# SSD scan of a hybrid encoder step: decay rows spread over the partitions by transfers from DRAM instead of matmuls, the decay matrix clamped and formed in place, the mask moved into the score block

## The chip, the cores and the metric

The kernel runs on one core of a Trainium2 chip. The metric is the device time of one execution in microseconds; it is given as the median of three runs. The engines are named as in the profile: PE (TensorE matmuls), PEld (TensorE weight loads), DVE (VectorE), ACT (ScalarE), POOL (GpSimd) and SP (SyncE, which issues the DMAs here).

## The reference, cut to what matters

The program is one inference step of a two-layer encoder: a Mamba-2 state-space (SSD) mixer with its FFN, then band attention with its FFN, in fp32, on 1024 prompt and 64 sample tokens of width 1024. Only the scan of the first layer is touched:

```python
dA = dt * A                                   # per token and head
Acs = jnp.cumsum(dA, axis=-1)                 # within a chunk
Lm = jnp.exp(jnp.where(causal, Acs[..., :, None] - Acs[..., None, :], -jnp.inf))
CB = jnp.einsum('bcqgn,bcsgn->bcgqs', Cc, Bc)
y_diag = jnp.einsum('bcgjqs,bcsgjp->bcqgjp', CB[:, :, :, None] * Lm, xd)
decay_to_end = jnp.moveaxis(jnp.exp(Acs[..., -1:] - Acs), -1, 2)
chunk_states = jnp.einsum('bcsgn,bcsgjp->cbgjpn', Bc, xd * decay_to_end[..., None])
h_final, h_prev = lax.scan(step, h0, (chunk_states, chunk_decay))   # h * d + s
y_off = jnp.einsum('bcqgn,cbgjpn->bcqgjp', Cc, h_prev) * jnp.moveaxis(jnp.exp(Acs), -1, 2)[..., None]
y = y_diag + y_off
```

There are 32 heads of 64 channels in 4 groups that share B and C, and a state of 128.

## The kernel before, in words

**Tiling.** The 1088 tokens are cut into three slices of 384, 384 and 320 columns, and a slice into chunks of 128 (nine in all, the last one of 64). Heads go in 16 pairs j, so a pair's 128 channels fill the partitions. A pair on a slice is a *unit* of the scan, numbered q = 3j + s: 48 units, 32 of 384 columns and 16 of 320.

**Main loop.** PE is filled by the input projection: tile by tile (z, x, B, C), eight k-steps of three passes, 24 matmuls in PSUM tile `mm` (L451 to L453), whose result DVE scales and moves out (`zs`, `craw`, L728). From x come the convolution and Silu (`xsT`, L766 to L776).

**Side tasks.** `table_task` (L683) makes the tables of dt and of the running sums `acs`, transposes the sums (`acT`, L715) and puts them as high and low parts into the rows `acr`; `cd` and `dec` are exponentials of them. `group_task` (L781) makes `Bn` and the score block `CB` of a group, copied from PSUM by ACT (L799). `ssd_task` (L809) is one unit: transposes `xtp` (L823); `xd` on DVE (L833), `xe` on POOL (L834); for each of the two heads a matmul `bcp` (L840) that spreads the head's row of running sums over all partitions (a selector column as weights, `acr` as the moving side); on DVE three operations that subtract the partition's own sum and take the minimum with a mask (L845); Exp of 64 rows for the state part (`ea`, L849) and of the matrix `dm` (L850) on ACT; `dm` times `CB` on DVE (L851). Then `sp`, the chunk states (L859), the state recurrence `hn` (L869, L872), `yp` from `dm` and `xd` (L889), `yo` from the states (L898), and the sum `y` (L900 to L903), which POOL multiplies by the gate z (L910) and SP stores to DRAM (L911). After a group's four pairs the sums of squares `ssg` (L921) are transposed (`nst`, L484) into a norm.

**What sets the order.** PE's order is written out by hand: a planner with a clock of its own (class `Stream`) lets main matmuls run, and puts a side task's next piece between them when its delay is over and its condition holds; a yield is (cost, delay, condition). So `SSD_D` and the numbers in the yields decide how many main matmuls stand between a unit's pieces. A tile of x is emitted only when the scan is near enough (L1077 and the lines after it: `so["C"] > q - 5`). The order on DVE, ACT, POOL and SP is made by the tile scheduler from priorities and buffers; each of these engines, and SP's queue, then takes its instructions strictly in order.

Of the kernel before, what the change touches and what calls it, by code (L numbers as in the profile page):

```python
# [8 lines left out]
F32 = mybir.dt.float32  # L9
F32R = mybir.dt.float32r  # L10
# [28 lines left out]

GAP_A, GAP_B = 1.8, 1.2  # L40
# [3 lines left out]
SSD_GAP, SSD_D = 4.4, 6.5  # L44
# [328 lines left out]
def hybrid_kernel(  # L373
# [34 lines left out]
    yd_ = dr.tile([P, XT, T], F32, name="yscr")  # L408
    od_ = dr.tile([P, KD, T], F32, name="oscr")
# [225 lines left out]
    with ExitStack() as es:  # L635
        pbc = es.enter_context(tc.tile_pool(reuse_waits="tile", name="pbc", bufs=2, space=PSUM))
        pyy = es.enter_context(tc.tile_pool(reuse_waits="tile", name="pyy", bufs=2, space=PSUM))
# [6 lines left out]
        mask = sb1.tile([P, P], F32, name="mask")  # L644
        G.memset(mask, BIG)
        G.affine_select(mask, mask, pattern=[[1, P]], compare_op=ALU.is_ge, fill=-BIG, base=0, channel_multiplier=-1)
# [3 lines left out]
        sel = sb1.tile([P, 32], F32R, name="sel")  # L650
        zero = sb1.tile([P, 1], F32, name="zero")
        G.memset(zero, 0.0)
        V.tensor_copy(sel[64:128, :], zero[64:128, :].to_broadcast([64, 32]))
        V.tensor_copy(sel[0:64, :], stk)
# [6 lines left out]
        acr = sb1.tile([P, T], F32R, name="acr")  # L661
        A.copy(acr[64:128, :], zero[64:128, :].to_broadcast([64, T]))
# [12 lines left out]
        dt, acs, dec, cd = tab("dt"), tab("acs"), tab("dec"), tab("cd")  # L675
# [7 lines left out]
        def table_task():  # L683
            ps = ax("dtn")
            for c in range(NCH):
                PE.matmul(ps[:, c * 32:(c + 1) * 32], dtT[c // 3][:64, (c % 3) * P:(c % 3 + 1) * P], stk, start=True, stop=True)
            with tc.high_priority(HIP):
                tt_ = [sb2.tile([P, 3, P], F32, tag=tg, bufs=2, name="tt") for tg in ("xe", "xe")]
                t0, t1 = (fl(t_)[:, :HW].rearrange("p (a b) -> p a b", b=HEADS) for t_ in tt_)
                t3 = dec  # L690
                V.tensor_tensor(t0, ps[:, :HW].rearrange("p (a b) -> p a b", b=HEADS), hb(pbs[:, 0:32]), op=ALU.add)
                V.scalar_tensor_tensor(fl(t1), fl(t0), -1.0, fl(t0), op0=ALU.mult, op1=ALU.min)
                A.activation(fl(t1), fl(t1), AF.Exp)
                V.tensor_scalar(fl(t3), fl(t1), LP[-1], None, op0=ALU.mult)
# [4 lines left out]
                V.scalar_tensor_tensor(t0, dt, -1.0, hb(negA), op0=ALU.mult, op1=ALU.mult)  # L699
            yield 1.0, TB_V  # L700
            pa = ax("acsp")
            PE.matmul(pa[:, :HW], U, fl(t0), start=True, stop=True)
            with tc.high_priority(HIP):
                V.tensor_copy(fl(acs), pa[:, :HW])
            yield 0.5, 1.0
            pl_ = ax("lastp")
            PE.matmul(pl_[:, :HW], ones, fl(t0), start=True, stop=True)

            with tc.high_priority(HIP):
                for s, (o, n) in enumerate(SL):  # L710
                    ps = (pyy, pyy, pbc)[s].tile([P, 512], F32, tag=("yy", "yy", "bc")[s], name="acT")
                    for i in range(3):
                        c = 3 * s + i
                        L = CHL[c]
                        PE.transpose(ps[:32, i * P:i * P + L], acs[:L, c, :], ident[:L, :L])  # L715
# [22 lines left out]
        class Conv:  # L738
# [5 lines left out]
            def __call__(self, s, ps_):  # L744
# [26 lines left out]
                if s < 2:  # L771
                    A.activation(dst[:, :384], dst[:, :384], AF.Silu)
# [8 lines left out]
        def group_task(g, s):  # L781
# [27 lines left out]
        def ssd_task(j, s):  # L809
# [5 lines left out]
            yield 0, 0, lambda: tabs and (g, s) in cb_done and so["A"] == q and so["C"] >= q - 1 and st.t >= so["tA"]  # L815
# [19 lines left out]
            MT = []  # L835
            ea = sb2.tile([P, 384], F32, tag="ea", name="ea")
            for e in range(2):
                hh = 2 * j + e
                bp = pbc.tile([P, 512], F32, tag="bc", name="bcp")
                PE.matmul(bp[:, :n], sel[:, hh:hh + 1].to_broadcast([P, P]), acr[:, o:o + n], start=True, stop=True)  # L840
                dm = sb2.tile([P, 384], F32, tag="dm", bufs=4, name="dm")
                for i in range(3):
                    c = 3 * s + i
                    L = CHL[c]
                    V.scalar_tensor_tensor(  # L845
                        dm[:, i * P:i * P + L], bp[:, i * P:i * P + L], acs[:, c, hh:hh + 1], mask[:, :L],
                        op0=ALU.subtract, op1=ALU.min,
                    )
                A.activation(ea[64 * e:64 * e + 64, :n], bp[64 * e:64 * e + 64, :n], AF.Exp)  # L849
                A.activation(dm[:, :n], dm[:, :n], AF.Exp)  # L850
                V.tensor_tensor(dm[:, :n], dm[:, :n], CB[:, :n], op=ALU.mult)  # L851
# [34 lines left out]
            for i in range(3):  # L886
                L = CHL[3 * s + i]
                for e in range(2):
                    PE.matmul(  # L889
                        yp[64 * e:64 * e + 64, i * P:i * P + L], xd[:, i, 64 * e:64 * e + 64],  # L890
                        MT[e][:, i * P:i * P + L], start=True, stop=True,
# [30 lines left out]
            if jj == 3:  # L922
                yield 0, 5.0
# [6 lines left out]
        def evac_of(kind, i):  # L930
# [32 lines left out]
        tags = [[], [("dm", 4)] * 4 + [("y", 6)] * 3 + [("ea", 2)], [("ea", 2)] + [("CT", 5)] * 2 + [("xd", 2)] * 2]  # L963
        for s, (o, n) in enumerate(SL):
# [14 lines left out]
            for m in range(KD):  # L979
                if m < len(tags[s]):  # L980
# [55 lines left out]
        for s in range(NSL):  # L1036
            us, n = u[s], SL[s][1]
            pl, tg = (pyy, "yy") if s == 1 else (pbc, "bc")
# [947 lines left out]
```

## Time and profile before

| | |
|---|---|
| Median of 3 runs | 2995.19 us (2993.03 to 2996.16) |
| Profiled execution | 2997.29 us, of which the span is 2995.6 us |
| Mean granted TensorE clock | 0.994 |
| Busy: PE, PEld | 2948.2 us (98%), 2891.8 us (97%) |
| Busy: DVE, ACT, POOL | 2044.8 us (68%), 1460.1 us (49%), 699.0 us (23%) |
| Scan's part of the span | about 87 to 660 us |

A row of the trace's timeline gives the start, the duration in us, engine, line, operation, `out<-in`, and how many instructions it sums up; what stands in brackets is idle time before it and who ended it. A row of the groups gives busy time and the mean in ns, then the idle time before. A row of waits gives the engine and its line, whom it waited for, us in total, how often, and the longest. Matmuls overlap, so a row's duration is longer than the distance to the next.

### The profile page before, as it was taken

To read this page: it belongs to the slowest core of one execution; us is meant where nothing else is said; L and a number is where in the kernel's file an instruction comes from. 1 tells how busy PE (TensorE), PEld (TensorE's weight loads), DVE (VectorE), ACT (ScalarE), POOL (GpSimd) and SP (SyncE) were. 2 spreads that over 40 slices of the span, in tenths; PEclk is the share of its full clock that TensorE was granted. 3 is DMA by queue.
4 is the path that set the end of the run, shared out by engine and by line. 5 is a ranking of instruction groups with operands and counts; after the bars stand their busy time and mean duration, and the time that the engine had idled before them with its cause. 6 is when DMAs were issued, how large, how long until landed. Compare 5 with 4: busy or idle time off the path is not lost.

```text
span 2995.6 us, 56513 instructions
## 1 busy us (share of the span) xinstructions
PE 2948.2 (98%) x21722; PEld 2891.8 (97%) x21722; DVE 2044.8 (68%) x4512; ACT 1460.1 (49%) x2643; POOL 699.0 (23%) x848
## 2 busy tenths in 40 slices
PE   8999999999999999999999999999999999999999
PEld 7999999999999999999999899999899999999999
DVE  7778887885768554574557778777778655475544
ACT  6756566564453232244445566555654322244443
POOL 1333333330121433351111000000131343451111
PEclk9999999999999999999999999999999999999999
DMA  3011111124654222255655222222356222245654
GB/s 122 33 59 51 61 50 49 61 68 145 192 150 141 83 73 80 76 161 173 202 177 169 87 76 79 70 65 86 116 171 188 80 76 77 80 148 176 214 179 136
DMA packets 180671, 335.43 MB, mean 112 GB/s; under 512 B 18192, under 2 KB 128400, under 8 KB 180400
## 3 DMA queue, kind: packets, MB, share of 16 engines
q1 hardware_dynamic: 178608, 325.45, 34.3%
q0 software_dynamic: 1792, 6.36, 1.1%
q8 instruction: 171, 2.80, 0.4%
q14 instruction: 100, 0.82, 0.1%
HBM read 264.69 MB, written 62.60 MB: 109 GB/s over the span
## 4 chain that ended last, share of the span: by engine, by line
PE 88%; DVE 7%; DMA 2%; ACT 2%; issue 1%; POOL 0%; SPq 0%; DVEq 0%; ACTq 0%; POOLq 0%
PE px L1264 9%; PE px L1265 9%; PE px L1266 9%; PE mm L451 8%; PE mm L453 8%; PE mm L452 8%; PE po L1464 6%; PE po L1465 6%; PE po L1463 6%; PE mmx L452 3%; PE mmx L451 3%; PE mmx L453 3%; PE po L1747 2%; PE ptp L1708 1%; PE yp L889 1%
## 5 line engine op out<-in xcount | busy, mean ns | idle before, releaser
L451 PE MATMUL mm<-r,hl 128*128 128x384 f32 (+2 forms) x1664 | 554.3, 333 | 6.4 <-DVE dt L698 3.4
L453 PE MATMUL mm<-r,hl 128*128 128x384 f32 (+2 forms) x1664 | 539.9, 324 | 3.2 <-DVE hl L351 2.6
L452 PE MATMUL mm<-r,hl 128*128 128x384 f32 (+2 forms) x1664 | 539.0, 324 | 0.0
L339 DVE TENSOR_TENSOR hl<-raw,hl 128x1024 fp32r<-128x1024 f32 (+1 forms) x219 | 260.6, 1191 | 219.9 <-ACT hl L338 217.3
L1265 PE MATMUL px<-r,hl 128*128 128x288 f32 (+1 forms) x1184 | 348.0, 294 | 0.0
L451 PEld LDWEIGHTS mm<-r,hl 128*128 128x128 f32 x1664 | 315.9, 190 | 9.0 <-ACT BT L775 3.7
L453 PEld LDWEIGHTS mm<-r,hl 128*128 128x128 f32 x1664 | 314.8, 189 | 4.6 <-DVE hl L351 3.7
L452 PEld LDWEIGHTS mm<-r,hl 128*128 128x128 f32 x1664 | 316.1, 190 | 0.0
L1264 PE MATMUL px<-r,hl 128*128 128x288 f32 x1056 | 311.3, 295 | 0.1
L1266 PE MATMUL px<-r,hl 128*128 128x288 f32 x1056 | 311.1, 295 | 0.0
L338 ACT CAST hl<-raw 128x1024 fp32r<-128x1024 f32 (+1 forms) x219 | 219.0, 1006 | 179.9 <-PE po L1465 97.1
L477 POOL TENSOR_TENSOR ssum<-ssum,sq 128x256 f32<-128x256 f32 (+3 forms) x97 | 128.4, 1324 | 640.6 <-ACT sq L476 625.3
L1265 PEld LDWEIGHTS px<-r,hl 128*128 128x128 f32 x1184 | 222.7, 188 | 0.0
L1266 PE MATMUL px<-rx,hl 128*128 128x256 f32 x768 | 216.5, 282 | 4.9 <-DVE hl L339 4.9
L1264 PE MATMUL px<-rx,hl 128*128 128x256 f32 x768 | 217.0, 283 | 0.6 <-ACT hl L338 0.6
L1464 PE MATMUL po<-rx,hl 128*128 128x384 f32 (+1 forms) x624 | 201.7, 323 | 0.1
L1264 PEld LDWEIGHTS px<-r,hl 128*128 128x128 f32 x1056 | 198.7, 188 | 0.5 <-DVE u L1279 0.5
L1266 PEld LDWEIGHTS px<-r,hl 128*128 128x128 f32 x1056 | 198.5, 188 | 0.0
L1463 PE MATMUL po<-rx,hl 128*128 128x384 f32 (+1 forms) x608 | 197.6, 325 | 0.0
L1465 PE MATMUL po<-rx,hl 128*128 128x384 f32 (+1 forms) x608 | 196.7, 323 | 0.0
L1265 PE MATMUL px<-rx,hl 128*128 128x256 f32 x640 | 180.1, 281 | 0.0
L288 POOL TENSOR_TENSOR tt<-raw 128x512 f32<-128x512 f32 x40 | 53.7, 1343 | 439.3 <-DMA raw<-in_w_f_dram 382.8
(367 smaller groups left out, 8163.3 us busy)
## 6 DMA issues: line engine op xcount, KB each, us to landing
raw<-in_w_f_dram SPq DMA_DIRECT2D x154, 512.0 KB, 3.8
rx<-in_w_f_dram SPq DMA_DIRECT2D x54, 512.0 KB, 3.6
raw<-in_w_in_dram SPq DMA_DIRECT2D x40, 512.0 KB, 3.5
sg<-hscr SPq DMA_DIRECT2D x88, 192.0 KB, 3.6
raw<-in_w_f_dram SPq DMA_DIRECT2D x44, 384.0 KB, 3.2
raw<-in_w_so_dram SPq DMA_DIRECT2D x32, 512.0 KB, 3.7
raw<-in_w_kv_dram SPq DMA_DIRECT2D x18, 512.0 KB, 3.5
raw<-in_w_o_dram SPq DMA_DIRECT2D x16, 512.0 KB, 3.6
```

The source lines that it names most:

```text
L338: self.nc.scalar.copy(h, v)
L339: (eng or self.eng or self.nc.vector).tensor_tensor(lo, v, h, op=ALU.subtract)
L451: PE.matmul(ps[:, :n], h_, xh, start=(first and i == 0), stop=False)
L452: PE.matmul(ps[:, :n], h_, xl, start=False, stop=False)
L453: PE.matmul(ps[:, :n], l_, xh, start=False, stop=(last and i == nk - 1))
L477: (eng or G).tensor_tensor(ssum[:, :n], ssum[:, :n], q[:, :n], op=ALU.add)
L1264: PE.matmul(ps, wh, ah[:, k, :], start=(k == 0), stop=False)
L1265: PE.matmul(ps, wh, al[:, k, :], start=False, stop=False)
L1266: PE.matmul(ps, wl, ah[:, k, :], start=False, stop=(k == 3))
L1463: PE.matmul(ps[:, :n], wh, xh, start=(k == 0), stop=False)
L1464: PE.matmul(ps[:, :n], wh, xl, start=False, stop=False)
L1465: PE.matmul(ps[:, :n], wl, xh, start=False, stop=(k == FT - 1))
```

## The change

The running sums are kept with the sign turned (`nac`). Their transposes are copied into rows by ACT and stored to a DRAM scratch `ascr` (32 heads by 1152). A unit then loads its two rows straight from there, spread over all 128 partitions (MT) and over 64 partitions each (`ea`). DVE forms the matrix in place, subtracting the partition's own sum and clamping at 0; ACT takes one Exp of the whole MT and one of `ea`, with a scale of −1. `CB` is multiplied by the triangular 0/1 mask `U` when DVE moves it out of PSUM, and MT by `CB` in one operation. The planner's numbers and the pools change with it.

```diff
-SSD_GAP, SSD_D = 4.4, 6.5
+SSD_GAP, SSD_D = 4.4, 8.0
...
+    ac_ = dr.tile([HEADS, NCH * P], F32, name="ascr")
...
-        pbc = es.enter_context(tc.tile_pool(reuse_waits="tile", name="pbc", bufs=2, space=PSUM))
-        pyy = es.enter_context(tc.tile_pool(reuse_waits="tile", name="pyy", bufs=2, space=PSUM))
+        pyy = es.enter_context(tc.tile_pool(reuse_waits="tile", name="pyy", bufs=4, space=PSUM))
...
-                        PE.transpose(ps[:32, i * P:i * P + L], acs[:L, c, :], ident[:L, :L])
-                    A.copy(acr[0:32, o:o + n], ps[:32, :n])
-                    V.tensor_tensor(acr[32:64, o:o + n], ps[:32, :n], acr[0:32, o:o + n], op=ALU.subtract)
-                V.tensor_tensor(fl(dec), pl_[:, :HW], fl(acs), op=ALU.subtract)
-                A.activation(fl(cd), pl_[:, :HW], AF.Exp)
+                        PE.transpose(ps[:32, i * P:(i + 1) * P], nac[:, c, :], ident)
+                    row = sb2.tile([P, 384], F32, tag="xd", name="row")
+                    A.copy(row[:32, :], ps[:32, :384])
+                    nc.sync.dma_start(ac_[:, o:o + 384], row[:32, :])
+                V.tensor_tensor(fl(dec), fl(nac), pl_[:, :HW], op=ALU.subtract)
+                A.activation(fl(cd), pl_[:, :HW], AF.Exp, scale=-1.0)
...
-                    G.memset(dst[:, 320:384], 0.0)
+                    A.activation(dst[:, 320:384], ident[:, 0:64], AF.Copy, scale=0.0)
...
-                L = CHL[3 * s + i]
-                PE.matmul(ps[:, i * P:i * P + L], BT[:, i * P:(i + 1) * P], CT[:, i * P:i * P + L], start=True, stop=True)
-            A.copy(CB[:, :n], ps[:, :n])
+                sl = slice(i * P, (i + 1) * P)
+                PE.matmul(ps[:, sl], BT[:, sl], CT[:, sl], start=True, stop=True)
+            V.tensor_tensor(
+                CB.rearrange("p (a b) -> p a b", b=P), ps[:, :384].rearrange("p (a b) -> p a b", b=P),
+                U.unsqueeze(1).to_broadcast([P, 3, P]), op=ALU.mult,
+            )
...
-            yield 0, 0, lambda: tabs and (g, s) in cb_done and so["A"] == q and so["C"] >= q - 1 and st.t >= so["tA"]
+            yield 0, 0, lambda: tabs and so["C"] >= q - 3
+            MT = sb2.tile([P, 2, 384], F32, tag="bp", bufs=4, name="MT")
+            row = ac_.offset + 2 * j * NCH * P + o
+            nc.sync.dma_start(MT, bass.AP(ac_.tensor, row, [[0, P], [NCH * P, 2], [1, 384]]))
+            ea = sb2.tile([P, 384], F32, tag="ea", bufs=3, name="ea")
+            for e in range(2):
+                nc.sync.dma_start(ea[64 * e:64 * e + 64, :n], bass.AP(ac_.tensor, row + e * NCH * P, [[0, 64], [1, n]]))
+            m3 = MT[:, :, :n]
+            for e in range(2):
+                for i in range(3):
+                    c = 3 * s + i
+                    m_ = MT[:, e, i * P:i * P + CHL[c]]
+                    last = V.tensor_scalar(m_, m_, nac[:, c, 2 * j + e:2 * j + e + 1], 0.0, op0=ALU.subtract, op1=ALU.max)
+            A.activation(m3, m3, AF.Exp, scale=-1.0)
+            x = A.activation(ea[:, :n], ea[:, :n], AF.Exp, scale=-1.0)
+            tc.add_manual_dep(x.ins, last.ins.name, AT, reason="one table load")
+            yield 0, SSD_D, lambda: (g, s) in cb_done and so["A"] == q and so["C"] >= q - 1 and st.t >= so["tA"]
...
-                PE.matmul(bp[:, :n], sel[:, hh:hh + 1].to_broadcast([P, P]), acr[:, o:o + n], start=True, stop=True)
...
-                A.activation(ea[64 * e:64 * e + 64, :n], bp[64 * e:64 * e + 64, :n], AF.Exp)
-                A.activation(dm[:, :n], dm[:, :n], AF.Exp)
-                V.tensor_tensor(dm[:, :n], dm[:, :n], CB[:, :n], op=ALU.mult)
-                MT.append(dm)
+            V.tensor_tensor(m3, m3, CB[:, :n].unsqueeze(1).to_broadcast([P, 2, n]), op=ALU.mult)
...
-            yield 0.7, 4.5, lambda: so["B"] == q
+            yield 0.35, 6.0, lambda: so["B"] == q
...
-                yield 0, 5.0
+                yield 0, 12.0 if g < 3 else 5.0
...
-                    st.spawn(ssd_task(i, s), SSD_D)
+                    st.spawn(ssd_task(i, s))
```

The rows `acr`, the selector `sel` and the additive `mask` are gone, and the staging tiles of the first layer's input take other buffers.

**How the order moves at the start of the scan.** First PE, from the transposes of units 0 and 1 to the third unit's, in the kernel before. `_1000`, `_1055` and `_1151` number the `xtp` tiles of units 0, 1 and 2; at each "..." 24 main matmuls are left out.

```order
L823 MATMUL xtp_1000<-ident_77,xsT_537 128x128 x3
L840 MATMUL bcp_1009<-acr_145,sel_134 128x384
L840 MATMUL bcp_1018<-acr_145,sel_134 128x384
...
L823 MATMUL xtp_1055<-ident_77,xsT_749 128x128 x3
L840 MATMUL bcp_1064<-acr_145,sel_134 128x384
L840 MATMUL bcp_1073<-acr_145,sel_134 128x384
L859 MATMUL sp_1082<-xe_1005,Bn_626 128x128 x3
...
L889 MATMUL yp_1122<-dm_1011,xd_1004 64x128
L889 MATMUL yp_1122<-dm_1020,xd_1004 64x128
```

In the changed kernel the same place on PE reads as follows, from its first row to its last without a main matmul between; 48 main matmuls of 384 columns and 24 of 320 stand between `acT` and the first `xtp`.

```order
L835 MATMUL xtp_1110<-ident_77,xsT_521 128x128 x3
L835 MATMUL xtp_1124<-ident_77,xsT_733 128x128 x3
L854 MATMUL sp_1133<-xe_1115,Bn_622 128x128 x3
L884 MATMUL yp_1145<-MT_1026,xd_1114 64x128 x6
L893 MATMUL yo_1152<-CT_510,hn_1137 128x128
L893 MATMUL yo_1152<-CT_510,hn_1139 128x128
L854 MATMUL sp_1159<-xe_1129,Bn_862 128x128 x3
L835 MATMUL xtp_1174<-ident_77,xsT_834 128x128 x3
```

The `bcp` rows are gone, and the two tiles of main matmuls that stood between the pieces of units 0 and 1 now stand ahead of them.

Next, SP at the same time in the changed kernel. `row` are the transposed sums of one slice, MT_987, MT_1000, MT_1013 and MT_1026 the matrices of units 1, 2, 3 and 0.

```order
L252 DMA raw_802<-in_w_in_dram 128x1024
L710 DMA ascr_109<-row_942 32x384
L710 DMA ascr_109<-row_949 32x384
L814 DMA MT_987<-ascr_109 128x2x384
L817 DMA ea_989<-ascr_109 64x384
L710 DMA ascr_109<-row_956 32x384
L817 DMA ea_989<-ascr_109 64x384
L814 DMA MT_1000<-ascr_109 128x2x384
L817 DMA ea_1002<-ascr_109 64x320 x2
L814 DMA MT_1013<-ascr_109 128x2x384
L817 DMA ea_1015<-ascr_109 64x384 x2
L814 DMA MT_1026<-ascr_109 128x2x384
```

Before, SP went from the weight rows `raw` straight to the stores of `y`; now three stores and these loads stand between, unit 0's matrix last.

Last, DVE in the changed kernel, from the last main tile ahead of the scan to the product that unit 0's `yp` reads.

```order
L721 TENSOR_TENSOR zs_1107<-mm_1082,rb2_145 128x320
L845 TENSOR_TENSOR xd_1114<-xtp_1110,dt_133 128x384
L845 TENSOR_TENSOR xd_1128<-xtp_1124,dt_133 128x384
L823 TENSOR_SCALAR MT_1026<-MT_1026,nac_134 128x128 x6
L864 COPY hn_1137<-sp_1133 128x128
L847 TENSOR_TENSOR MT_1000<-MT_1000,CB_963 128x2x320
L867 SCALAR_TENSOR_TENSOR hn_1139<-hn_1137,cd_136,sp_1133 128x64 x2
L867 SCALAR_TENSOR_TENSOR hn_1142<-hn_1139,cd_136,sp_1133 128x64 x2
L847 TENSOR_TENSOR MT_1013<-MT_1013,CB_623 128x768
L847 TENSOR_TENSOR MT_1026<-MT_1026,CB_623 128x768
```

Before, each unit's subtractions and products stood right behind its own `xd`; here the products of units 2 and 3 stand ahead of unit 0's.

More of the change, by code (lines that the diff above doesn't have):

```diff
@@ L38 @@
 EPS = 1e-6
+AT = mybir.DependencyInfo(mybir.DependencyClass.Sync, mybir.DependencyReason.DATA)
 GAP_A, GAP_B = 1.8, 1.2
@@ L673, in hb @@
             return ap.unsqueeze(1).to_broadcast([P, NCH, HEADS])
-        dt, acs, dec, cd = tab("dt"), tab("acs"), tab("dec"), tab("cd")
+        dt, nac, dec, cd = tab("dt"), tab("nac"), tab("dec"), tab("cd")
         tabs = []
@@ L703, in table_task @@
             with tc.high_priority(HIP):
-                V.tensor_copy(fl(acs), pa[:, :HW])
+                V.tensor_copy(fl(nac), pa[:, :HW])
             yield 0.5, 1.0
@@ L710, in table_task @@
                 for s, (o, n) in enumerate(SL):
-                    ps = (pyy, pyy, pbc)[s].tile([P, 512], F32, tag=("yy", "yy", "bc")[s], name="acT")
+                    ps = pyy.tile([P, 512], F32, tag="yy", name="acT")
                     for i in range(3):
@@ L834, in ssd_task @@
             G.tensor_tensor(hd(xe), hd(xd), tb(dec), op=ALU.mult)
[L835 to L851, printed above, removed]
-                MT.append(dm)
+            V.tensor_tensor(m3, m3, CB[:, :n].unsqueeze(1).to_broadcast([P, 2, n]), op=ALU.mult)
             so["A"] = q + 1
             so["tA"] = st.t + SSD_GAP
-            yield 0.7, 4.5, lambda: so["B"] == q
+            yield 0.35, 6.0, lambda: so["B"] == q
             sp = ax("sp")
@@ L979, in hybrid_kernel @@
             for m in range(KD):
-                if m < len(tags[s]):
+                if s == 1 and m < 4:
+                    if m % 2 == 0:
+                        x2 = sb2.tile([P, 2, 384], F32, tag="bp", bufs=4, name="x0")
+                    xt = x2[:, m % 2, :n]
+                elif m < len(tags[s]):
                     xt = sb2.tile([P, 384], F32, tag=tags[s][m][0], bufs=tags[s][m][1], name="x0")[:, :n]
```

18 lines of the change are left out of this document (4 added, 14 removed).

## The prediction, on record before the result

> **What bounds the kernel now.** I read the first part of the page, then its chain, then a table of stretches, and last what TensorE waits for in the state-space stage, where all of the change lies.
>
> ```profile
> span 2995.6 us, 56513 instructions
> PE 2948.2 (98%) x21722; PEld 2891.8 (97%) x21722; DVE 2044.8 (68%) x4512; ACT 1460.1 (49%) x2643; POOL 699.0 (23%) x848
> PE 88%; DVE 7%; DMA 2%; ACT 2%; issue 1%; POOL 0%; SPq 0%; DVEq 0%; ACTq 0%; POOLq 0%
> 80.00:180.00 100.00, 97.85 (x699) 92.15 (x698) 83.39 (x227) 71.92 (x109) 35.58 (x58) 1.00 0.13 43
> 180.00:640.00 460.00, 460.00 (x3201) 446.71 (x3202) 371.01 (x966) 281.54 (x443) 150.43 (x289) 1.00 0.17 55
> PE bcp L840 <- ACT ea L849: 2.6, 4, 1.3
> PE nst L484 <- DVE ssg L921: 5.4, 3, 3.2
> ```
>
> Lines four and five are stretches of the span: the stretch, its length, then busy time of PE, PEld, DVE, ACT and POOL, granted clock, DMA share and GB/s. From 180 to 640 us PE is busy for 460.0 of 460.0 us, with DVE at 371 (81%) and ACT at 282 (61%). A matmul taken out there comes off the time one to one, as long as nothing makes PE wait instead. The last two lines are PE's waits from 80 to 660 and from 640 to 700 us: it loses 2.6 us for the PSUM bank of a spread row, and 5.4 us at the stage's end for the group sums.
>
> **What goes.** Each of 48 units (pair j, slice s) spreads two decay rows by one matmul each.
>
> ```profile
> L840 PE MATMUL bcp<-acr,sel 128*128 128x384 f32 x64 | 19.6, 383 | 0.4 <-ACT ea L849 0.3
> L840 PE MATMUL bcp<-acr,sel 128*128 128x320 f32 x32 | 9.2, 358 | 2.4 <-ACT ea L849 2.3
> 262.50 0.42 PE L451 MATMUL mm<-r,hl 128*128 128x384 f32 x1
> 262.76 0.34 PE L452 MATMUL mm<-r,hl 128*128 128x384 f32 x1
> ...
> 264.49 0.33 PE L453 MATMUL mm<-r,hl 128*128 128x384 f32 x1
> 264.67 0.31 PE L451 MATMUL mm<-r,hl 128*128 128x320 f32 x1
> ...
> 266.27 0.31 PE L453 MATMUL mm<-r,hl 128*128 128x320 f32 x1
> ...
> 268.11 0.60 PE L840 MATMUL bcp<-acr,sel 128*128 128x384 f32 x2
> 268.55 0.30 PE L451 MATMUL mm<-r,hl 128*128 128x320 f32 x1
> ```
>
> The 383 ns of the group is not the price, since matmuls overlap; the distance between starts is. From 262.76 to 264.49 ten main matmuls of 384 columns start, 1.73 us, so 0.173 each; from 264.67 to 266.27 eleven of 320, 0.145 each. The first matmul after a small fp32 piece costs 262.76 − 262.50 = 0.26, that is 0.09 more, a restart. The two spread rows at 268.11 hold PE for 0.44: two slots of 0.173 and one such restart. The restart stays, because the main matmuls then follow the transposes `xtp` directly. So 64 × 0.173 + 32 × 0.145 = 15.7 us go, and I take **−15.7**; if the restarts went too, 48 × 0.09 = 4.3 more, so the end is −20. With the PSUM bank goes its wait: **−2.6**. Five small matmuls widened to 128 columns, at 0.1 or less each, cost +0.2.
>
> **DVE, ACT and POOL in a full stage** do not end the path if their sums stay under PE's.
>
> ```profile
> L845 DVE SCALAR_TENSOR_TENSOR dm<-bcp,acs,mask 128x128 f32<-128x128 f32 x256 | 72.6, 342 | 0.0
> L1693 DVE TENSOR_SCALAR sc<-sc,mx 128x128 f32<-128x128 f32 x16 | 4.5, 285 | 0.5
> L849 ACT ACT_TABLE_LOAD x48 | 61.6, 1283 | 29.1 <-DVE dm L845 28.4 <-issue 0.3
> 88.06 0.56 DVE L833 TENSOR_TENSOR xd<-xtp,dt 128x384 f32<-128x384 f32 x1
> 88.54 1.64 DVE L845 SCALAR_TENSOR_TENSOR dm<-bcp,acs,mask 128x128 f32<-128x128 f32 x6
> 92.15 0.56 DVE L851 TENSOR_TENSOR dm<-dm,CB 128x384 f32<-128x384 f32 x1 [1.10 <-ACT dm L850]
> ```
>
> A unit's mask-and-subtract takes 1.64 us and its two products with CB 2 × 0.56: 2.76. After, six TENSOR_SCALARs by the 128-column row of the attention stage take at most 6 × 0.285 = 1.71, and one product of 768 columns about 1.0: 2.7, DVE unchanged, plus 12 × 0.56 = 6.7 us in all for the mask that moves into CB. That is under 2% of the 460. ACT trades four Exps for two wider ones and gets 16 more table loads, 16 × 1.283 = 20.5 us over 560, which its 39% of idle time hides; POOL loses 24 memsets. I cost all this at **0**. Without that cover, 6.7 + 20.5 = 27 would be the most, and only if both stood ahead of PE every time.
>
> **The transfers in the full stage.** 48 loads of 384 KB and 96 of 64 rows are 28.3 MB, or 49 GB/s over 580 us beside the 55 of the row above. A unit's load is emitted when the scan's output of four units earlier is, three units and more ahead of its use; a unit has two main tiles of 24 matmuls, 48 × 0.16 = 7.7 us, so that is over 23 us.
>
> ```profile
> raw<-in_w_in_dram SPq DMA_DIRECT2D x32, 512.0 KB, 3.5
> yscr<-y SPq DMA_DIRECT2D x14, 160.0 KB, 2.0
> SPq L911 <- POOL y L910: 182.7, 30, 31.0
> 109.68 0.33 SPq L911 DMA_DIRECT2D yscr<-y  x1
> ```
>
> A 512 KB load lands 3.5 us after its issue, a store of 160 KB after 2.0, so 23 us cover both: **0**. SP issues 147 DMAs more at 0.33, 49 us of a queue that mostly waits for its producers (third line). What stands behind those waits is the rival below.
>
> **The start of the scan** is where I expect a bill. In the order of before, 24 main matmuls stand between the first units' transposes and between each transpose and its `yp`. Now the first two units' transposes, `sp`, `yp`, `yo`, the second `sp` and the third `xtp` stand in one run without a main matmul, because the two tiles that covered them have moved ahead of the first `xtp`. So PE waits openly for what `yp` needs: MT_1026, the last of four loads on SP.
>
> ```profile
> 83.51 1.20 PE L715 MATMUL acT<-ident,acs 128*32 128x128 f32 x9
> ...
> 87.50 0.53 PE L823 MATMUL xtp<-ident,xsT 128*128 128x128 f32 x3
> ...
> 97.66 0.88 PE L889 MATMUL yp<-dm,xd 128*64 128x128 f32 x12
> 98.46 0.71 PE L898 MATMUL yo<-CT,hn 128*128 128x128 f32 x4
> 99.01 0.83 PE L859 MATMUL sp<-xe,Bn 128*128 128x128 f32 x6
> 99.68 0.49 PE L823 MATMUL xtp<-ident,xsT 128*128 128x128 f32 x3
> 89.38 0.52 ACT L772 ACTIVATE xsT<-xsT 128x384 f32<-128x384 f32 x1
> 88.77 0.83 POOL L834 TENSOR_TENSOR xe<-xd,dec 128x384 f32<-128x384 f32 x1 [4.39 <-DVE xd L833]
> 95.40 0.28 DVE L869 COPY hn<-sp 128x128 f32<-128x128 f32 x1
> ```
>
> PE: `acT` ends near 84.7; the small pieces of B and C and their restarts take 0.8, then 48 × 0.173 + 24 × 0.145 = 11.8 of main matmuls, so the first `xtp` starts near 97.2 (87.50 before) and both are done at 97.7. The load: ACT's copy of the third row stands behind the Silu that ends at 89.9, is done near 90.4, its store lands 0.33 + 2.0 later (92.7), seven issues of 0.33 bring MT_1026's to an end at 95.0, and with 3.5 it lands near 98.5. DVE, in its order: two `xd` to 98.9, six TENSOR_SCALARs 1.7 (100.6), the copy of `hn` 0.3, the product of MT_1000 0.9, two updates of `hn` 1.1, the products of MT_1013 and MT_1026 1.0 each: 104.9. Then `yp` 0.80, `yo` 0.55, `sp` 0.67 and `xtp` 0.25 (the distances above), and main matmuls again at 107.2. Of these 10.0 us PE works 3.4, and idles 6.6; I take **+6.5**. The low end is 5: six such operations took 1.64 where six means are 2.05, an overlap that takes 0.3 off the TENSOR_SCALARs and as much off the products, with some 0.8 for PE's and DVE's hand-overs that I counted twice. The high end is 12, if the four loads' 1.5 MB share what one 512 KB load moves in 3.5 us, 150 GB/s: 10.3 us from 92.7, 4.5 later than 98.5, and 1 of queueing. [...]
>
> The next units have 12 main matmuls, 2.1 us, between `xtp` and `sp`, where `xd` (0.56) and `xe` (0.83) with hand-overs take 2 or a little more: **+0.6**, between 0 and 3. The stage's end keeps its 5.4 us, which the last group's sums make on DVE: **0**, between −2 and +2.
>
> **Sum.** −15.7 − 2.6 + 0.2 + 6.5 + 0.6 = −11.0, against the profiled execution's 2997.29 us (its span of 2995.6 and 1.7 around it). That execution stands 2.1 above the median of the three runs, 2995.19; by the median, 2984.2. I predict **2984**. The ends of the terms give 2976 (−20 − 2.6 + 0.2 + 5 + 0 − 2) and 2994 (−15.7 − 2.6 + 0.2 + 12 + 3 + 2); inside them the forecast's own range is 2979 to 2991.
>
> **Rivals.**
> - *The start costs its upper end* and the tight units 3: −15.7 − 2.6 + 0.2 + 12 + 3 = −3.1, so **2992**, and 2989 to 2999 if both run over. For it: four loads at once, DVE has 0.8 of its time taken already. Against: the first of the four is issued before the third row's store and lands while that is under way. Chance 0.14.
> - *DVE stands still behind a load* (slower). DVE takes its instructions in order, so a TENSOR_SCALAR whose MT has not landed holds up the evacuation of the two main PSUM tiles behind it. SP is in order too, and a load behind a store of `y` inherits its wait for POOL: 182.7 us in 30 waits, 6.1 on average, the longest 31.0. PE has 24 main matmuls, 4.2 us, in hand. From the point where a load lands more than 4.2 us after DVE reaches it, PE stops: 6.1 − 4.2 = 1.9 a time. One unit in three has a store directly ahead, 16 × 1.9 = +30 on the forecast: **3014**. Against: 23 us of lead over a mean wait of 6.1. Chance 0.13.
> - *More is gained*: the restarts go too (−4.3) and the start costs 5: 2984.2 − 4.3 − 1.5 = **2978**. Against: the restart follows any small fp32 piece. Chance 0.10.
> - That the rows are still spread on PE is excluded: the order of the changed program holds no `bcp` row.
>
> **Chances.** The forecast has 0.63. The bound of 0.2%, 6.0 us, is about what a measurement of this kernel can tell from no change: 2989.2 to 3001.2. Of the forecast 0.58 lie under it and 0.05 within; the first rival is within but for 0.01; the second is slower; the third faster. Faster 0.69, same 0.18, slower 0.13. The range from 2976 to 2999 leaves out the slower rival and a part of the first and the third, under 0.2.
>
> **What would show it.** Waits of PE between 97 and 107 us: `yp` on DVE's product of MT for 3 to 4 us and `sp` on POOL's `xe` for about 2; no wait on `ea`. The stretch from 180 to 640 as full as before, and the stage's last row about 11 us earlier. Right for the cover: DVE waits for MT's loads only near 98 us. A row of DVE waiting for MT from DMA in the full stage, with main matmuls behind a PSUM tile, would show the slower rival. TENSOR_SCALARs over 0.35 us, or POOL's multiplications growing beside them, would raise the tight units. I am wrong in the main point if PE's busy time in the stage does not fall by about 16.

## The result, and the profile after

The changed kernel takes 2993.13 us in the median, the kernel before 2996.22 us in runs beside it: a ratio of 0.9989, with a 95% interval from 0.998 to 0.9999. That is 3 us gained where 11 were forecast. One run of twelve was disturbed and stays out of the ratio. The page of the changed kernel begins:

```profile
span 2993.4 us, 56388 instructions
PE 2935.9 (98%) x21626; PEld 2878.7 (96%) x21626; DVE 2039.4 (68%) x4471; ACT 1450.9 (48%) x2574; POOL 709.0 (24%) x821
```

PE is busy for 12.3 us less (2948.2 before), yet the span is only 2.2 us shorter. Four stretches of the changed kernel (PE, PEld, DVE, ACT, POOL busy, then the granted clock, DMA share, GB/s) and PE's waits from 83 to 700 us show where the rest went:

```profile
83.00:125.00 42.00, 33.88 (x218) 32.10 (x216) 30.50 (x80) 24.83 (x33) 7.21 (x11) 0.88 0.32 96
125.00:180.00 55.00, 52.98 (x379) 49.93 (x379) 49.45 (x128) 40.90 (x55) 28.24 (x39) 0.97 0.44 134
180.00:640.00 460.00, 458.50 (x3197) 443.84 (x3197) 374.95 (x954) 286.12 (x405) 158.49 (x277) 1.00 0.32 100
640.00:700.00 60.00, 53.94 (x405) 51.12 (x404) 49.30 (x133) 29.68 (x62) 11.44 (x15) 0.97 0.41 119
```

```profile
PE sp L854 <- POOL xe L846: 4.4, 1, 4.4
PE yp L884 <- DVE MT L847: 3.8, 1, 3.8
PE nbp L517 <- DVE xd L845: 2.7, 1, 2.7
PE nbp L517 <- DVE nv L498: 2.2, 2, 1.4
PE xtp L835 <- DVE nv L498: 1.3, 3, 0.4
PE sp L854 <- ACT rb L520: 1.0, 1, 1.0
PE xtp L835 <- ACT xsT L767: 1.0, 1, 1.0
PE xtp L835 <- ACT xsT L769: 0.8, 1, 0.8
```

The full stage is as full as forecast (458.5 of 460), and no wait on `ea` from a PSUM bank is left. The scan's start shows the two waits that were forecast, and the column behind them what was not: the granted clock is 0.88 there and 0.97 behind it.

**A measuring rod.** The time of a whole execution varies by 3 us and more, and the head of the program, ahead of the scan, by up to 6 us from profile to profile. So I measure each profile between two events of its own, from the start of `lastp`, two matmuls of the tables ahead of the scan's start (83.03 us before, 82.92 after), to the first `px` of the FFN (951.6 and 949.8). In slices of 1 us I add up what PE was not busy (**idle**) and, of its busy time, what the clock took (busy times one minus the granted clock: **half clock**). What is left is PE's own work. The medians are of 5 to 12 runs, but for the kernel that ran once; each ratio is to runs of the kernel before beside them.

| kernel | median, us | ratio to before (95%) | lastp to px | idle | half clock | rest |
|---|---|---|---|---|---|---|
| before | 2996.22 | | 868.6 | 10.0 | 1.6 | 857.0 |
| changed | 2993.13 | 0.9989 (0.998 to 0.9999) | 866.9 | 18.8 | 6.6 | 841.5 |
| spreads left out (of before) | 2991.04 | 0.9983 (0.9974 to 0.9992) | 863.4 | 17.6 | 3.3 | 842.5 |
| spreads of 32 columns (of before) | 2993.28 | 0.9989 (0.998 to 0.9998) | 867.9 | 11.8 | 3.3 | 852.8 |
| load order | 2992.13 | 0.9987 (0.9978 to 0.9995) | 868.3 | 17.8 | 9.1 | 841.4 |
| fill 44 + 40 | 2998.36 | 1.0008 (1.0 to 1.0017) | 873.9 | 10.2 | 3.2 | 860.5 |
| fill 18 + 16 | 2990.04 (one run) | | 863.7 | 12.4 | 1.7 | 849.6 |
| cover | 2988.28 | 0.9976 (0.9966 to 0.9985) | 860.3 | 14.5 | 3.4 | 842.4 |
| cover and fill 16 | 2989.48 | 0.9975 (0.9964 to 0.9986) | 863.1 | 12.4 | 5.7 | 845.0 |
| stores by POOL | 2997.36 | 1.0003 (0.9994 to 1.0012) | 870.0 | 19.8 | 6.7 | 843.5 |
| order, cover, POOL | 2999.48 | 1.0008 (0.9999 to 1.0017) | 870.6 | 19.6 | 6.5 | 844.5 |
| old planner numbers | 3004.34 | 1.0027 (1.0017 to 1.0037) | 877.5 | 28.8 | 3.4 | 845.3 |
| four ea | 2983.60 | 0.9962 (0.9948 to 0.9975) | 857.1 | 13.6 | 2.5 | 841.0 |
| order, four ea | 2980.72 | 0.9952 (0.994 to 0.9965) | 856.7 | 10.6 | 5.4 | 840.7 |

The last column is the check on the rod: without fill it stays within 840.7 and 845.3 for every kernel that has no spreading matmuls. Counted from the kernel before, rod and median have the same sign in every row, but they differ by up to 4.4 us (order, four ea: −11.9 and −16.3). No kernel was profiled twice, so a difference of a few us between two rods is not shown to be more than noise. From before to changed the rest falls by 15.5, and idle and half clock rise by 8.8 and 5.0: 1.7 us are left.

### The profile page after: what moved, and what is told of

Its sections match the earlier page's. It is cut to its first block, busy times and chain, and to the rows that moved or that the text cites. A ratio compares the mean times of both kernels' runs of the same rounds, so it can differ in the third digit from the quotient of the medians.

```text
span 2993.4 us, 56388 instructions
## 1 busy us (share of the span) xinstructions
PE 2935.9 (98%) x21626; PEld 2878.7 (96%) x21626; DVE 2039.4 (68%) x4471; ACT 1450.9 (48%) x2574; POOL 709.0 (24%) x821
## 4 chain that ended last, share of the span: by engine, by line
PE 83%; DVE 9%; DMA 4%; ACT 2%; issue 2%; POOL 0%; SPq 0%; DVEq 0%; ACTq 0%; POOLq 0%
PE px L1263 9%; PE px L1265 9%; PE px L1264 9%; PE mm L454 7%; PE mm L456 7%; PE mm L455 7%; PE po L1463 6%; PE po L1464 6%; PE po L1462 6%; PE mmx L455 3%; PE mmx L454 3%; PE mmx L456 3%; PE po L1746 2%; PE ptp L1707 1%; PE yp L884 1%
```

## The experiments

**Is the removed work worth what I said?** The kernel before, without its spreading matmuls:

```diff
-                bp = pbc.tile([P, 512], F32, tag="bc", name="bcp")
-                PE.matmul(bp[:, :n], sel[:, hh:hh + 1].to_broadcast([P, P]), acr[:, o:o + n], start=True, stop=True)
...
-                        dm[:, i * P:i * P + L], bp[:, i * P:i * P + L], acs[:, c, hh:hh + 1], mask[:, :L],
+                        dm[:, i * P:i * P + L], acs[:, c, hh:hh + 1].to_broadcast([P, L]), acs[:, c, hh:hh + 1], mask[:, :L],
...
-                A.activation(ea[64 * e:64 * e + 64, :n], bp[64 * e:64 * e + 64, :n], AF.Exp)
+                A.activation(ea[64 * e:64 * e + 64, :n], acs[64 * e:64 * e + 64, 3 * s, hh:hh + 1].to_broadcast([64, n]), AF.Exp)
```

> The kernel before, with its 96 spreading matmuls left out and nothing in their place: DVE subtracts a sum from itself and ACT takes Exp of a column, both spread from SBUF, so the decay matrix is a wrong one and the scan's output with it. It measures the removed term by itself. Theory A: 64 x 0.173 + 32 x 0.145 = 15.7 us and the 2.6 us of waits for the PSUM bank go, -18 us against the kernel before (2996 to 2978). Theory B (PE does not set the stage's length): less than 5 us.

It gained 5.5 us, between the two theories. The rest fell by 14.5, near the 15.7 of the slots, and 9.3 us came back, 7.6 as idle time and 1.7 as half clock. Its full stage, and PE's waits from 120 to 660 us:

```profile
180.00:640.00 460.00, 456.01 (x3180) 440.96 (x3181) 398.84 (x984) 336.30 (x485) 171.22 (x297) 1.00 0.18 55
```

```profile
PE nst L484 <- POOL ssg L919: 4.0, 5, 1.1
PE xtp L823 <- ACT xsT L772: 2.5, 2, 1.6
PE xtp L823 <- ACT xsT L774: 2.4, 1, 2.4
```

In the full stage it is `nst` that waits, for POOL's sums; the waits of `xtp` for ACT's Silu lie ahead of 180 us. ACT is busy for 336 of 460 us instead of 282. Between 80 and 660 us this program has 140 table loads where before has 98: as I read it, nothing keeps a unit's Exps together without the matmul. So the next kernel kept every instruction and shortened only the matmul, of which DVE and ACT then read one column over and over:

```diff
-                PE.matmul(bp[:, :n], sel[:, hh:hh + 1].to_broadcast([P, P]), acr[:, o:o + n], start=True, stop=True)
+                PE.matmul(bp[:, :32], sel[:, hh:hh + 1].to_broadcast([P, P]), acr[:, o + 96:o + 128], start=True, stop=True)
...
-                        dm[:, i * P:i * P + L], bp[:, i * P:i * P + L], acs[:, c, hh:hh + 1], mask[:, :L],
+                        dm[:, i * P:i * P + L], bp[:, 31:32].to_broadcast([P, L]), acs[:, 3 * s, hh:hh + 1], mask[:, :L],
...
-                A.activation(ea[64 * e:64 * e + 64, :n], bp[64 * e:64 * e + 64, :n], AF.Exp)
+                A.activation(ea[64 * e:64 * e + 64, :n], bp[64 * e:64 * e + 64, 31:32].to_broadcast([64, n]), AF.Exp)
```

> The kernel before with its 96 spreading matmuls cut to 32 columns, of which DVE and ACT read one over and over, so the decay matrix is a wrong one and the scan's output with it; every instruction, dependence and table load stays in its place. It asks whether the waits of the run without spreading matmuls came from its 32 added table loads. Theory A (they did; the removed PE time is a gain wherever the order stays): PE idle and clock loss up to the next stage stay near the 13.4 and 3.8 us of before, and the first matmul of the next stage comes earlier by what the shorter matmuls save, 8 to 13 us. Theory C (the order is laid so tightly around PE's own work that any shortening comes back as waits): idle time above 18 us and less than 5 us gained.

Table loads were 98 again. I had the saving too high: two spreads of 32 columns still hold PE for 0.22 us instead of 0.44, and the restart behind them (0.085) comes on top, so the rest fell by 4.2 only. Idle and half clock rose by 3.5, of which 1.7 is half clock behind 1.9 us of waits near 118 us (the kernel before waits 1.8 us at 121 to 123 us and loses none), so the rod is 0.7 us shorter; the medians differ by 3.2 (2993.28 against 2996.44 beside it). Theory A's 8 to 13 us did not come, nor did theory C's idle time above 18 us. The first run shows that before was laid so close to the data that PE time saved is not wholly time gained. How much of the 4.2 came back here, 3.5 us by the rod or 1 by the medians, is not settled, and so neither is the part that the table loads had in the first run's waits.

**What did the start cost, idle time or clock?** Identity matmuls into a spare PSUM tile, in both waits of unit 0, 44 and 40 of them, then 18 and 16:

```diff
+            if q == 0:
+                dmy = pyy.tile([P, 512], F32, tag="yy", name="dmy")
+                for _ in range(18):
+                    PE.matmul(dmy[:, :P], ident, ident, start=True, stop=True)
             sp = ax("sp")
...
+            if q == 0:
+                for _ in range(16):
+                    PE.matmul(dmy[:, :P], ident, ident, start=True, stop=True)
             yp = pyy.tile([P, 512], F32, tag="yy", name="yp")
```

> The changed kernel with 44 matmuls of the identity, whose result nobody reads, ahead of unit 0's sp and 40 ahead of its yp, so that PE is busy in both waits. Theory A with the clock as part of the bill: the waits end at the same times (sp near 102.4, yp near 107.5 us), the granted clock stays at 1.0, yp to the next main matmul takes 2.3 us instead of 4.3, and with half a us behind it the whole is -2.6 us against the changed kernel. Rival (only the idle time costs, the clock would have come back anyway): yp to the next main matmul stays at 4.3 and the time within 0.5 us.

> The changed kernel with 18 and 16 identity matmuls of 0.23 us in the two waits at the scan's start, a third of the time they took with 44 and 40. Theory A with the clock: sp near 102.4 and yp near 107.5 us as in the changed kernel, granted clock 1.0 there, main matmuls again near 109.8 instead of 111.8, and no half clock behind. Rival: 111.8.

The first was sized wrongly: a matmul took 0.228 us, so 84 are 19.2 us, and the rest rose by 19.0; it cost 5 us. Half clock on the rod is 3.2 us against the changed kernel's 6.6, less by about what the start had lost there, as theory A had it, but without a gain. The second, with 7.8 us, fitted into the waits. PE's side tasks at its start (the fills have two rows for a matmul), and the clock there:

```profile
95.99 0.82 PE L836 MATMUL xtp<-ident,xsT 128*128 128x128 f32 x6
96.64 4.18 PE L856 MATMUL dmy<-ident 128*128 128x128 f32 x36
100.66 0.83 PE L859 MATMUL sp<-xe,Bn 128*128 128x128 f32 x6
101.33 3.74 PE L887 MATMUL dmy<-ident 128*128 128x128 f32 x32
105.00 0.88 PE L892 MATMUL yp<-MT,xd 128*64 128x128 f32 x12
```

```profile
102.00:106.00 4.00, 4.00 (x41) 3.71 (x40) 3.75 (x9) 1.67 (x2) 0.00 (x0) 1.00 0.00 0
106.00:110.00 4.00, 4.00 (x32) 4.00 (x32) 2.24 (x8) 0.00 (x0) 0.83 (x1) 1.00 0.72 232
```

From the first `xtp` to the next main matmul it took 11.3 us (95.99 to 107.26), against 14.55 in the changed kernel, and the rod is 3.2 us shorter; 2.6 us were expected of the first fill. Not all of it is the clock: in this run the load that stands ahead of `xd` on DVE landed sooner, so `xd` began 1.8 us behind the first `xtp` (97.82) instead of 3.6. What is the clock's own is the same work in less time: `sp` took 0.83 us instead of 1.34, and `yp` to the next main matmul 2.3 (105.00 to 107.26) instead of 4.3. So in this run work that computes nothing kept the clock at 1.00, and the half clock was a bill of its own; that it made the whole kernel faster rests on one run.

**Does the order of the loads or missing cover make the waits?** Loads in the order of the units, and in another kernel a sixth x buffer:

```diff
-            yield 0, 0, lambda: tabs and so["C"] >= q - 3
+            yield 0, 0, lambda: tabs and so["C"] >= q - 3 and so["L"] == q
+            so["L"] = q + 1
```

> The changed kernel with one more condition, so that the units' loads are emitted in the order 0, 1, 2, 3 instead of 1, 2, 3, 0. Theory A (what the removed matmuls gave was given back where the scan starts, by waits without cover and by a clock that falls to half in them): yp of unit 0 no longer waits for the product of the last load, so the 3.75 us wait before it goes, while the 4.4 us wait of sp on xe stays (xd still stands behind the fourth load on DVE); main matmuls again near 108 us instead of 111.8, the whole -4 us (-2.5 to -5.5) against the changed kernel's 2993. Theory B (the loads slow the full stage and the start costs nothing that matters): within 1 us of 2993.

```diff
-                    self.prev = sb2.tile([P, 4], F32, tag="halo", bufs=6, name="halo")
+                    self.prev = sb2.tile([P, 4], F32, tag="halo", bufs=5, name="halo")
...
-                cvx = pair_t[i] = Conv(i, "xsT", 5)
+                cvx = pair_t[i] = Conv(i, "xsT", 6)
...
-                    st.wait_for(lambda: so["C"] > q - 5)
+                    st.wait_for(lambda: so["C"] > q - 6)
```

> The changed kernel with a sixth buffer for the x tiles (one halo buffer less) and x allowed one tile further ahead, so that 24 main matmuls stand between the transposes of units 0 and 1; the loads keep their order. Theory A: these 24 matmuls, 3.5 to 4.2 us, fill most of the 4.4 us wait of sp; the 3.75 us wait of yp stays and the clock falls only there; -4 us (-2 to -6) against the changed kernel. Theory B: within 1 us.

The order alone gained nothing that shows (rod +1.3, median −1.0): the wait of `yp` went, but the other grew to 5.75 us. The clock was at half for 10.2 us, as long as in the changed kernel, with more of PE's work in it (4.0 us lost instead of 3.2). PE's rows, then two of DVE's:

```profile
98.95 1.65 PE L855 MATMUL sp<-xe,Bn 128*128 128x128 f32 x6 [5.75 <-POOL xe L847]
100.53 1.55 PE L885 MATMUL yp<-MT,xd 128*64 128x128 f32 x12
```

```profile
91.29 1.27 DVE L824 TENSOR_SCALAR MT<-MT,nac 128x128 f32<-128x128 f32 x6 [4.65 <-DMA MT<-ascr]
...
97.36 1.02 DVE L846 TENSOR_TENSOR xd<-xtp,dt 128x384 f32<-128x384 f32 x2
```

The load for the first of these rows had landed by then, but DVE had stood 4.65 us for it, and what it had to make up without a gap (three sets of subtractions, two products and two main tiles) all came ahead of `xd`, and so of `xe`. The first `px` of this profile came 3.5 us earlier, as expected, but its `lastp` came 4.9 earlier too; by the absolute time I would have called it a success. The cover gained 6.5 us on the rod, 4 to 5 in the medians: the wait of `sp` went, that of `yp` (3.9 us) stayed. A fill of 16 in that wait as well:

> The run with the sixth x buffer, with 16 identity matmuls ahead of unit 0's yp, 3.7 us of work in the 3.9 us wait that was left there. If the half clock behind that wait costs by itself: no clock loss between 83 and 125 us (1.7 us before), the next stage's first matmul near 940.7 instead of 942.4, time 2986 to 2987. If it does not: 942.4 and 2988.

It took the clock loss at the start away (1.7 to 0 us) and the idle time (3.9 to 0.3 us), but the fill is 3.7 us itself, and half clock came in other places, between 125 and 180 us and at the end (5.7 us there, 1.7 in the run with the cover alone). The medians, 2989.48 and 2988.28, do not differ by more than their intervals. What the fill was to show at its place, it showed; the gain did not come.

**The second stall.** The rows of ACT around 156 us in the changed kernel, ACT's wait from 112 to 180 us and that of SP from 130 to 165 us, then PE:

```profile
156.26 0.47 ACT L825 ACTIVATE ea<-ea 128x320 f32<-128x320 f32 x1 [2.91 <-DMA ea<-ascr]
156.74 1.28 ACT L767 ACT_TABLE_LOAD   x1
158.04 0.42 ACT L767 ACTIVATE xsT<-xsT 128x256 f32<-128x256 f32 x1
```

```profile
ACT ea L825 <- DMA ea<-ascr: 5.2, 3, 2.9
```

```profile
SPq L906 <- POOL y L905: 9.1, 4, 5.4
SPq L817 <- POOL y L898: 7.1, 4, 3.2
```

```profile
158.51 0.44 PE L835 MATMUL xtp<-ident,xsT 128*128 128x128 f32 x2 [0.99 <-ACT xsT L767]
159.75 0.33 PE L835 MATMUL xtp<-ident,xsT 128*128 128x128 f32 x1 [0.80 <-ACT xsT L769]
...
161.07 0.53 PE L454 MATMUL mm<-r,hl 128*128 128x384 f32 x1
```

ACT stands 2.91 us before the Exp of `ea`, the Silu of x behind it, and `xtp` behind that; then the main matmuls run at half clock (0.50 from 160.84 to 164.25 us), 0.32 us apart instead of 0.17. Two waits of SP can have made the load late: the store of `y` ahead of it (L906), or the buffer that POOL still reads (L898). The stores were moved to POOL's queue first:

```diff
-            nc.sync.dma_start(yd_[:, j, o:o + n], y[:, :n])
+            nc.gpsimd.dma_start(yd_[:, j, o:o + n], y[:, :n])
```

> The changed kernel with the 48 stores of y issued by POOL instead of SP, nothing else. Theory A: the wait of ACT for the row ea near 156 us, behind which the Silu of x stands, comes from a load queued on SP behind a store that waits for POOL; it goes, and with it the two waits of xtp near 158 us (1.8 us) and 1.7 us of half clock: -3 us (-1 to -4) against the changed kernel, the start as it was. Rival (issuing costs POOL more than it saves): xe comes later, waits of sp on xe appear in the full stage, and the time is 2993 or above.

The waits of `ea` stayed (ACT 4.8 us in 3, 2.2 at most, in the same stretch), so the store was not the cause, and the kernel was no faster, 2997.36. The rival's time came, but not its waits: in the full stage no `sp` waits for `xe`. Why it is 4 us slower than the changed kernel is open; each of the 48 issues took POOL 0.56 us. A kernel with this, the order and the cover together fared no better, and theory A failed there: the rod is 3.7 us longer than the changed kernel's and 10 longer than that of the cover alone.

> The changed kernel with three edits together: loads in the order of the units, a sixth x buffer so that 24 main matmuls stand between the transposes of units 0 and 1, and the stores of y issued by POOL, which makes y, instead of SP. Theory A (the gain went into waits and half clock at the scan's start and near 157 us): PE's idle time between 83 and 180 us falls from 10.1 to under 4 us and the 4.9 us lost there to the clock go, so the first matmul of the next stage comes 8 to 13 us earlier than in the changed kernel (949.8) and the time falls to 2980 to 2985. Rival (something else in the stage is as late, so that waits come back elsewhere before 700 us): no more than the sixth buffer gives alone, 2988.

Then the buffer:

```diff
-            ea = sb2.tile([P, 384], F32, tag="ea", bufs=3, name="ea")
+            ea = sb2.tile([P, 384], F32, tag="ea", bufs=4, name="ea")
...
-                    self.prev = sb2.tile([P, 4], F32, tag="halo", bufs=6, name="halo")
+                    self.prev = sb2.tile([P, 4], F32, tag="halo", bufs=5, name="halo")
```

> The changed kernel with a fourth buffer for the rows ea (one halo buffer less), nothing else. In the changed kernel SP holds the load of ea until POOL has added an older ea into y, and ACT, in order, holds the Silu of x behind the Exp of that row (2.9 us near 153 us). Theory D (that buffer makes the second stall): the waits of xtp near 158 us (1.8 us) and the 1.7 us of half clock behind them go, ACT waits for ea's loads no longer between 112 and 180 us, the next stage's first matmul comes at 946 to 948 instead of 949.8, -3.5 us (-2 to -5). Rival E (the load is late because SP's queue is long, whatever the buffers): no change, within 1 us.

> The changed kernel with the loads in the order of the units and the fourth ea buffer. If the two stalls are separate, their gains up to the next stage add: 3.5 us of the order (949.8 to 946.3 in that run) and 3.5 of the buffer, first matmul of the next stage near 943, time near 2987. If one only moves the other along, near 946 and 2991.

No wait of ACT for `ea` is left in the stretch, and the two stretches that it touches became:

```profile
125.00:180.00 55.00, 55.00 (x406) 52.18 (x405) 50.89 (x134) 39.12 (x53) 26.88 (x36) 1.00 0.41 122
640.00:700.00 60.00, 55.84 (x444) 53.58 (x443) 42.94 (x114) 25.13 (x57) 9.07 (x10) 1.00 0.40 122
```

Idle 2.0 and half clock 1.7 between 125 and 180 us are gone, 3.7 us as expected; theory D holds against E. (The halo buffer is not the reason: the cover gave up the same one, and PE idled 2.5 us there.) The kernel gained more than that, 9.8 us on the rod: 3.6 at the stage's end (1.9 idle, 1.7 clock), where PE no longer waits for `rb`, and 1.6 at the start, which I had not foreseen. With the load order on top the rod is 0.4 shorter, so nothing shows that the two add; the medians, 2980.72 and 2983.60, have overlapping intervals. Both beat the kernel before and the changed one by more than their intervals: 0.9952 and 0.9962 to 0.9989.

**The planner's numbers.** Three of them put back, SSD_D 6.5, 4.5 ahead of `sp` and 5.0 ahead of the group norm:

> The changed kernel with three planner numbers put back to those of before (SSD_D 6.5, 4.5 ahead of sp, 5.0 ahead of the group norm). It asks whether the new numbers make the start. 12 main matmuls then stand between the transposes of units 0 and 1, and sp comes sooner behind xtp everywhere. Theory A: 2 us less idle at the start; in the full stage sp then waits for xe now and then; in all between -2 and +3 us of 2993. If the numbers do not matter: within 1 us of 2993.

It is 7 us slower than before, 11 slower than the changed kernel, so the numbers matter more than I thought. At the start 1.3 us of idle time and 1.5 of half clock went, near the 2 of theory A, but the full stage idles 12.1 us:

```profile
180.00:640.00 460.00, 447.86 (x3098) 430.10 (x3096) 367.22 (x928) 278.33 (x395) 161.01 (x268) 1.00 0.31 96
```

```profile
PE nst L487 <- POOL ssg L916: 5.9, 3, 2.0
PE xtp L835 <- ACT xsT L765: 2.7, 6, 0.6
```

`nst` waits for the sums because its delay is short again, and `xtp` for the Silu because a unit starts 1.5 planner us sooner; this is read from the waits, since the three were put back together. Together these delays keep the changed kernel's full stage full.

## Why the prediction was wrong, step by step

- **The removed matmuls: right.** −15.7 and +0.2 were forecast; the rest of the rod fell by 15.5.
- **The bank's waits: right.** 2.1 of the 2.2 us that PE idled between 83 and 180 us went with the wait for `ea`'s bank.
- **The start: the step that failed, in size.** The term of +6.5 us came out at 11.3: 8.1 of idle time, and 3.2 of half clock, which had no term. The forecast had the first `xtp` at 97.2 (97.25 came), `yp` at 104.9 (107.53) and 6.5 us of idle time. PE's and DVE's rows there:

```profile
97.25 0.82 PE L835 MATMUL xtp<-ident,xsT 128*128 128x128 f32 x6
102.43 1.34 PE L854 MATMUL sp<-xe,Bn 128*128 128x128 f32 x6 [4.36 <-POOL xe L846]
107.53 1.55 PE L884 MATMUL yp<-MT,xd 128*64 128x128 f32 x12 [3.75 <-DVE MT L847]
109.00 1.22 PE L893 MATMUL yo<-CT,hn 128*128 128x128 f32 x4
110.02 1.49 PE L854 MATMUL sp<-xe,Bn 128*128 128x128 f32 x6
111.30 0.85 PE L835 MATMUL xtp<-ident,xsT 128*128 128x128 f32 x3
```

```profile
99.26 1.27 DVE L823 TENSOR_SCALAR MT<-MT,nac 128x128 f32<-128x128 f32 x6 [1.81 <-DMA MT<-ascr]
100.44 0.49 DVE L721 TENSOR_TENSOR zs<-mm,rb 128x320 f32<-128x320 f32 x1
100.84 1.02 DVE L845 TENSOR_TENSOR xd<-xtp,dt 128x384 f32<-128x384 f32 x2
101.77 2.26 DVE L823 TENSOR_SCALAR MT<-MT,nac 128x128 f32<-128x128 f32 x6
```

  I put both `xd` at 97.8 and did not ask what stands ahead of them on DVE: the subtraction of MT_1013, whose load landed at 99.2. So `xd` began at 100.84, 3 us late, and `xe` with it. The load was late by itself, too: by the forecast's figures (the fourth of seven issues of 0.33 behind 92.7, and 3.5 to land) it lands at 97.5. SP ended that issue at 94.95, and the load took 4.3 us more. The six subtractions of unit 0 took 2.26, not 1.7, with POOL's `xe` beside them (101.55 to 103.2).
- **The clock: not in the sum at all.** From 102.8 to 113.05 us the granted clock is 0.5. `yp` to the first main matmul took 4.3 us (107.53 to 111.80) where the sum had 2.27. In all 3.2 us here and 1.7 behind the stall at 157 us: 4.9 of the 9.3 us by which the rod missed the forecast of −11. The prediction gives no reason for leaving it out. The kernel before had none between 83 and 640 us, where PE idled 2.2 us in all and 1.3 at most at a time.
- **Full stage at nothing: wrong in one place.** From 180 to 640 us DVE did wait for MT's loads, 18.8 us in 20 waits, and PE never felt it, so the slower rival did not come about on DVE. ACT waited too, for `ea`, the load that I had not looked at, and PE felt that once, at 157 us: 2.0 us idle and 1.7 of clock. I had cost 23 us of lead; the lead ended where the buffer did, with three units, not with the load's condition.
- **Tight units, +0.6:** 1.5 us of idle time in the full stage, mostly `xtp` behind the norm's read of a PSUM bank (1.3 us), not the hand-over that I named.
- **The stage's end at 0:** −0.6 us, idle and clock, though other instructions wait there now.

The sum of the rod: −15.5 + 9.2 at the start (8.1 + 3.2 − 2.1) + 3.6 at 157 us + 1.5 − 0.6 + 0.1 = −1.7. The first rival had nearly the right size, 12 against 11.3 for the start, but by luck. It had the four loads share their bandwidth until MT_1026 lands at 103.0; they landed 3.5 to 4.9 us behind the start of their issues, MT_1026 at 100.64, before DVE began the first `xd`. What made the size was one load ahead of `xd`, and the clock. What no run here settles is how much of the cover's gain would add to that of the fourth buffer: no run has both.

## What to carry to other kernels

Where PE is the bound, price a wait as the idle time and what the clock takes behind it (8.1 and 3.2 us at this start), and ask for each wait which instructions stand ahead of the one you wait for on its own engine. A load that is issued early is only as early as its buffer is free: SP stood 7.1 us in 4 waits for that of `ea`. And time a change from one local event to another: the head of the program alone moved by 6 us between profiles. But each kernel here has one profile, so the noise of the rod itself is not known.

## What the runs showed of the hardware that I had not expected

The same idle time of PE was not always the same bill: half clock came behind some waits and not behind others. Stretches of the changed kernel, each 3.41 us long, the length of its shortest half clock between 83 and 700 us:

```profile
99.40:102.81 3.41, 0.38 (x3) 0.38 (x4) 3.41 (x11) 2.23 (x3) 1.26 (x2) 1.00 0.07 25
102.81:106.22 3.41, 0.96 (x5) 0.67 (x4) 3.41 (x12) 3.37 (x5) 0.36 (x1) 0.50 0.00 0
...
109.64:113.05 3.41, 3.41 (x17) 3.41 (x17) 1.60 (x8) 0.00 (x0) 0.00 (x0) 0.50 0.78 267
113.05:116.46 3.41, 3.41 (x29) 3.22 (x30) 2.33 (x8) 1.14 (x2) 0.89 (x1) 1.00 0.00 0
...
157.42:160.84 3.42, 1.62 (x10) 1.30 (x10) 1.92 (x6) 3.39 (x7) 0.65 (x1) 1.00 0.47 180
160.84:164.25 3.41, 3.41 (x12) 3.41 (x11) 3.41 (x11) 2.14 (x4) 3.02 (x5) 0.50 0.48 130
```

At the start the clock fell 4.7 us after PE had stopped (98.07 to 102.81) and came back 5.5 us after `yp` began (107.53 to 113.05). From 84 to 930 us the changed kernel was at half clock three times, for 10.24 us from 102.81 and for 3.41 us from 160.84 and from 659.18, the kernel before once, for 3.41 us from 679.03. In the 3.41 us ahead of these falls PE idled 3.04, 1.80, 2.58 and 2.87 us. The fall at 160.84 did not follow one long wait: PE was busy for 1.62 of the 3.41 us ahead of it, between waits of 0.99 and 0.80 us. Elsewhere PE idled as much or more without a fall. Between 125 and 180 us the changed kernel idled 2.0 us at a clock of 0.97, but the second fill 4.1 and the run without spreads 4.2 us, both at 1.00:

```profile
125.00:180.00 55.00, 50.89 (x368) 47.69 (x367) 47.31 (x121) 37.76 (x52) 24.31 (x34) 1.00 0.41 124
125.00:180.00 55.00, 50.77 (x368) 48.03 (x369) 49.84 (x124) 40.35 (x60) 27.19 (x35) 1.00 0.14 45
```

So idle time of this size cost nothing more or 1.7 us, and what decides it stays open here. That much luck is in each figure of half clock above, the 1.7 of the second stall included.

A subtraction on DVE took 0.28 us in the median and up to 1.09 us. The 47 that had an operation of POOL beside them for over 90% of their time took 0.86 us in the median, the 200 that had none at most 0.29. But no run took POOL away, so that POOL is the cause is a reading and not shown.
